# Keys, values and the sample's probabilities: transposed by TensorE, or in 32 by 32 blocks by VectorE with DMAs through DRAM

## The chip, the cores and the metric

The kernel runs on one core of a Trainium2 chip. The metric is device time in microseconds (us) of one execution. Engines are named as the profile names them: PE (TensorE's matmuls), PEld (its weight loads), DVE (VectorE), ACT (ScalarE), POOL (GpSimd), SP (SyncE, which only issues DMAs).

## What is computed

One layer of a decoder on 256 prompt tokens and 8 samples of 8 tokens, all of width 2048:

```
z = RMSNorm(x) @ W_in      # [B | C | h | q | k | v | gate_conv | gate_attn]
y_A = (B * conv3(C * h)) @ W_conv_out
y_B = attention(q, k, v) @ W_attn_out      # 16 query heads, 4 key/value heads of 64, window 128,
                                           # relative bias, a sink in the softmax's denominator
x = x + (sigmoid(gate_conv) * y_A + sigmoid(gate_attn) * y_B) @ W_o
x = x + SwiGLU(RMSNorm(x)); y = RMSNorm(x)
```

The prompt attends within itself; each sample attends to 128 cached keys and values and to its own 8 new ones. Besides y, the last 128 keys and values of the prompt and of each sample are outputs, row by row (a token's keys side by side).

## The kernel before, in words

The activations lie transposed, a feature to a partition and the 320 tokens along the row. Each weight matrix streams from DRAM in tiles of 128 x 1024 floats (four blocks of 128 rows by 256 columns; SP issues the loads, four buffers). Each weight tile is split into two parts, the upper one by ACT (whi, L129) and the lower one by DVE (wlo, L130), three buffers each, and gives PE 24 matmuls with 320 columns (L186, in the helper `product`): upper weights by upper activations, upper by lower, lower by upper. The order of the products is: keys and values together (L376), four of q, then four times C, H and B for the short convolution, then eight times gate_conv, gate_attn, W_conv_out and W_attn_out, then W_o, then the gate and up products and the down products.

Attention is side work. It is written as generators; `product` calls `tick` after each weight tile, and `tick` runs the generator to its next `yield`. So a `yield` puts what follows it behind one more weight tile of PE work (24 matmuls). The instructions that a tick emits stand behind the latest weight split and matmul on ACT, DVE and PE (`issue_after`); apart from that, a planner that works from its own estimates of durations puts each engine's instructions in order, so POOL's queue need not follow the order of the code. `nudge` (L207) is a single matmul whose result nobody uses.

While the q products run, `kv_work` runs: the first norm (`first_norm`, which scales vT and kT, L456), then `kv_natural` for three groups of tokens (128, 128, 64), a yield behind each, then `keys_twice`. `kv_natural(t)` turns values (L502) and, for the second and third group, keys (L505) from feature-major to token-major by PE: 2, 4 and 4 transpositions of 128 x 128 or 128 x 64 into the PSUM tile pk. DVE copies them out to vn (L506) and kn (L509), and POOL's queue issues DMAs of the outputs (L511 to L515). vn is then the stationary operand of the products of probabilities and values (L611 for the prompt, L726 for the sample's new tokens).

While C, H and B run, `attention` runs: the prompt's eight units, then the sample. The sample's probabilities lie in s_s (L701: divided by their sum), rows of heads and queries, for each sample 128 cached and 8 new keys. One tick takes a copy of the new part (pnew, L703). The next has eight PE transpositions of the cached part into spp (L709), copied by ACT to ptw (L710), one of the new part into spn (L712), copied by DVE to pns (L714), and then DVE spreads pns over the samples (ptn, L716). Two yields later PE multiplies by the new values (L726) and by the cached ones (L736) into spo, and a tick after that ACT and DVE take spo to at_t (L621, L622).

The convolution's small steps share POOL: copies into ue and out to g (L811, L812, L818, L819) and products with the norm (L829, L830). ACT (L822) and DVE (L824) do the rest of it.

Of the kernel before, what the change touches and what calls it, by code (L numbers as in the profile page):

```python
# [8 lines left out]
F32 = mybir.dt.float32  # L9
F32R = mybir.dt.float32r  # L10
AF = mybir.ActivationFunctionType
ALU = mybir.AluOpType
# [3 lines left out]
D = 2048  # L16
TP, NB, TS = 256, 8, 8
T = TP + NB * TS
DC = 1024
NH, NKV, HD, GRP = 16, 4, 64, 4  # L20
DKV = NKV * HD
WIN = 128
# [4 lines left out]
P = 128  # L27
# [21 lines left out]
TOK = [(0, 128), (128, 128), (256, 64)]  # L49
# [3 lines left out]
def hybrid_layer(ctx: ExitStack, tc: tile.TileContext, a: dict, o: list):  # L53
    nc = tc.nc
    y_0, y_r, nk_p, nv_p, nk_s, nv_s, ncv = o

    w_in, w_kv, w_co, w_ao, w_o, w_g, w_u, w_d = (
        a[n] for n in ("w_in", "w_kv", "w_conv_out", "w_attn_out", "w_o", "w_gate", "w_up", "w_down")
    )
# [7 lines left out]
    dr = ctx.enter_context(tc.tile_pool(name="dr", bufs=1, space=bass.MemoryType.DRAM))  # L67
# [4 lines left out]
    def ps_aux(name):  # L72
        return aux[0].tile([P, 512], F32, tag="aux", name=name)
# [3 lines left out]
    def u(s):  # L77
        uid[0] += 1
        return f"{s}_{uid[0]}"
# [133 lines left out]
    def flip(ap):  # L213

        *rest, (step, n) = ap.ap
        return bass.AP(ap.tensor, ap.offset + (n - 1) * step, [*rest, (-step, n)])


    ident = cst.tile([P, P], F32, name="ident")
    ones = cst.tile([P, 1], F32, name="ones")  # L220
# [8 lines left out]
    blk = cst.tile([64, NB], F32, name="blk")  # L229
# [47 lines left out]
    kT = zz.tile([P, 2, T], F32, name="kT")  # L277
    vT = zz.tile([P, 2, T], F32, name="vT")
    vn = [zz.tile([P, DKV], F32, name=f"vn{t}") for t in range(3)]
# [198 lines left out]
    pr = pr_p.enter_context(tc.tile_pool(name="pr", bufs=1, side="right"))  # L478
# [16 lines left out]
        return at_t[:, o:o + TP]  # L495


    def kv_natural(t):
        t0, tn = TOK[t]
        pk = ps_aux(u("pk"))  # L500
        for j in range(2):
            nc.tensor.transpose(pk[:tn, j * P:(j + 1) * P], vT[:, j, t0:t0 + tn], ident)  # L502
        if t > 0:
            for j in range(2):
                nc.tensor.transpose(pk[:tn, 256 + j * P:256 + (j + 1) * P], kT[:, j, t0:t0 + tn], ident)  # L505
        nc.vector.tensor_copy(vn[t][:tn, :], pk[:tn, 0:DKV])  # L506
        if t > 0:
            kn = pr.tile([P, 4, WIN], F32, tag="s", name=u("kn"), bufs=3).rearrange("p g k -> p (g k)")[:, :DKV]
            nc.vector.tensor_copy(kn[:tn, :], pk[:tn, 256:512])  # L509
            if t == 1:  # L510
                nc.gpsimd.dma_start(nk_p[0, 0].rearrange("t h d -> t (h d)"), kn)  # L511
                nc.gpsimd.dma_start(nv_p[0, 0].rearrange("t h d -> t (h d)"), vn[1])
            else:
                for dst, s in ((nk_s, kn), (nv_s, vn[2])):
                    nc.gpsimd.dma_start(  # L515
                        dst[0, :, WIN - TS:WIN].rearrange("b t h d -> b t (h d)"), s[:tn, :]
                    )

    def cache_shift():

# [128 lines left out]
    def sample_attention(sm):  # L649
        kf = sm.tile([P, NB, 2, W2], F32, name="kf")  # L650
        for h in range(0, NB, 2):
            nc.gpsimd.dma_start(kf[:, h:h + 2, :, 0:WIN], a["cache_kt"][:, h:h + 2])
        s = sm.tile([P, NB, W2], F32, name="s_s")
        yield
        new = kT[:, :, TP:T].rearrange("p j (b t) -> p b j t", b=NB)
        for j in range(2):
            nc.scalar.activation(kf[:, :, j, WIN:W2], new[:, :, j], AF.Copy)
        yield
        yield
        for base in range(0, NB, 3):  # L660
            ps = ps_aux(u("pss"))
            n = min(3, NB - base)
            for b in range(base, base + n):
                o0 = (b - base) * W2
                for kv in range(NKV):
                    j, par = kv // 2, kv % 2
                    rows = slice(par * 64, par * 64 + 64)
                    nc.tensor.matmul(
                        ps[kv * 32:(kv + 1) * 32, o0:o0 + W2], qs[rows, j, b, :], kf[rows, b, j, :],
                        start=True, stop=True,  # L670
                    )
            nc.vector.tensor_add(
                s[:, base:base + n, :], ps[:, 0:n * W2].rearrange("p (b k) -> p b k", b=n),
                flip(bias_s).unsqueeze(1).to_broadcast([P, n, W2]),
            )
        yield
        yield

        def vals(b):
            cv = sm.tile([P, DKV], F32, tag="ckv", name=u("cv"), bufs=8)  # L680
            nc.gpsimd.dma_start(cv, a["cache_v"][0, b].rearrange("t h d -> t (h d)"))
            return cv

        cvs = {b: vals(b) for b in range(NB)}
        mx = wk.tile([P, NB], F32, tag="smx", name="smx")
        den = wk.tile([P, NB], F32, tag="sden", name="sden")
        es = wk.tile([P, NB], F32, tag="ses", name="ses")
        nc.vector.tensor_reduce(mx, s, axis=AX.X, op=ALU.max)
        nc.vector.tensor_scalar(mx, mx, sink_s, -1.0, op0=ALU.max, op1=ALU.mult)
        nc.vector.tensor_scalar(es, mx, sink_s, None, op0=ALU.add)  # L690
        yield
        for b in range(NB):
            nc.scalar.activation(
                s[:, b, :], s[:, b, :], AF.Exp, bias=mx[:, b:b + 1], accum_out=den[:, b:b + 1]
            )
        nc.scalar.activation(es, es, AF.Exp)
        yield
        nc.vector.tensor_add(den, den, es)
        nc.vector.reciprocal(den, den)
        for b in range(NB):  # L700
            nc.vector.tensor_scalar(s[:, b, :], s[:, b, :], den[:, b:b + 1], None, op0=ALU.mult)  # L701
        pn = sm.tile([P, NB, TS], F32, name="pnew")
        nc.vector.tensor_copy(pn, s[:, :, WIN:W2])  # L703
        yield
        ptw = sm.tile([P, NB * P], F32, name="ptw")
        for h in range(2):
            pp = ps_aux(u("spp"))
            for i in range(4):
                nc.tensor.transpose(pp[:, i * P:(i + 1) * P], s[:, h * 4 + i, 0:WIN], ident)  # L709
            nc.scalar.activation(ptw[:, h * 512:(h + 1) * 512], pp, AF.Copy)  # L710
        pp = ps_aux(u("spn"))
        nc.tensor.transpose(pp[:64, 0:P], pn.rearrange("p b k -> p (b k)"), ident)  # L712
        pns = sm.tile([64, P], F32, name="pns")
        nc.vector.tensor_copy(pns, pp[:64, 0:P])  # L714
        ptn = sm.tile([64, NB, P], F32, name="ptn")
        nc.vector.tensor_tensor(  # L716
            ptn, pns.unsqueeze(1).to_broadcast([64, NB, P]), blk.unsqueeze(2).to_broadcast([64, NB, P]),
            op=ALU.mult,
        )
        yield  # L720
        yield
        pos = [ps_aux(u("spo")) for _ in range(2)]
        for j in range(2):
            for par in range(2):
                kv = j * 2 + par
                nc.tensor.matmul(  # L726
                    pos[j][par * 64:(par + 1) * 64, 0:256].rearrange("p (b r) -> p b r", b=NB),
                    vn[2][:64, kv * HD:(kv + 1) * HD], ptn[:, :, kv * 32:(kv + 1) * 32],
                    start=True, stop=False,
                )  # L730
        for b in range(NB):
            cv = cvs.pop(b)
            for j in range(2):
                for par in range(2):
                    kv = j * 2 + par
                    nc.tensor.matmul(  # L736
                        pos[j][par * 64:(par + 1) * 64, b * 32:(b + 1) * 32],
                        cv[:, kv * HD:(kv + 1) * HD], ptw[:, b * P + kv * 32:b * P + (kv + 1) * 32],
                        start=False, stop=(b == NB - 1),
                    )  # L740
        yield
        for j in range(2):
            src = pos[j][:, 0:256].rearrange("p (b g t) -> p g b t", b=NB, g=GRP)
            o = LEAD_A + j * 4 * at_row
            rows = at_t[:, o:o + 4 * at_row].rearrange("p (g w) -> p g w", g=GRP)[:, :, -2 * JS:]
            two_to(*(rows[:, :, c:c + JS].rearrange("p g (b t) -> p g b t", b=NB) for c in (0, JS)), src)
        yield
# [10 lines left out]

    def kv_work():
        yield from first_norm()  # L760
        for t in range(3):
            kv_natural(t)
            yield
        yield from keys_twice()

    def attention():
# [31 lines left out]
    for cp in range(4):  # L798
        c_sb = []
        ps = in_pair(O_C + cp * CW, "C")  # L800
        for c in range(2):
            t = tmp("ta", "csb")
# [4 lines left out]
        for c in range(2):  # L807
# [12 lines left out]
            cv = tmp("tc", "cv")  # L820
            n = UL - 2
# [11 lines left out]
        for c in range(2):  # L833
            ch = cp * 2 + c
            cv, cs = conv[c]
            t = tmp("td", "bc")
# [23 lines left out]
    for mp in range(8):  # L860
        c0 = mp * CW
        sg = {}
        for nm, off, tag in (("gc", O_GC, "ta"), ("ga", O_GA, "tb")):
            ps = in_pair(off + c0, nm)
            for c in range(2):
                t = tmp(tag, nm)[:, :T]
# [12 lines left out]
        for c in range(2):  # L879
            t = sg["ga", c]  # L880
# [394 lines left out]
```

## Time and profile before

| | |
|---|---|
| time, median of 3 runs | 1600.82 us (1600.62 to 1601.08) |
| profiled execution, first to last instruction | 1598.6 us |
| what lies around the span, by the median | 2.2 us |
| DVE busy | 884.0 us, 55% |
| ACT busy | 650.6 us, 41% |
| POOL busy | 78.3 us, 5% |
| HBM read and written | 253.30 MB, 5.08 MB |

The profile has no time of its own execution but its span; the median comes from runs without it. In rows of groups, "x8" is a count, then come the busy time of the group in us, the mean ns of one, and the idle time before them with what ended it. The chain in order of time lists, for each piece of the work that ended last, its start, its length, its engine, its output's name, its line and a count. DMA rows give KB each and the median us from issue to landing.

### The profile page before, as it was taken

How to read it: one execution, taken by the hardware profiler on the slowest of the kernel's cores; microseconds unless marked ns; L12 is line 12 of the kernel's file. 1: busy time of each engine (PE TensorE's matmuls, PEld its weight loads, DVE VectorE, ACT ScalarE, POOL GpSimd, SP SyncE). 2: the span in 40 equal slices, each digit the busy share in tenths (PEclk: the TensorE clock that was granted, in tenths of full speed). 3: DMA queues.
4: the chain of work that ended last, by engine and by line, in shares of the span. 5: the costliest groups of instructions: out<-in, count | busy, mean ns of one | idle time of the engine just before them, and what ended most of it. 6: DMA issues, size and time to landing. Idle time of an engine off the chain costs nothing.

```text
span 1598.6 us, 26406 instructions
## 1 busy us (share of the span) xinstructions
PE 1590.2 (99%) x10957; PEld 1554.8 (97%) x10957; DVE 884.0 (55%) x1315; ACT 650.6 (41%) x928; POOL 78.3 (5%) x123
## 2 busy tenths in 40 slices
PE   9999999999999999999999999999999999999998
PEld 9999999999999999999999999998888999999887
DVE  7879565445555545556555555553444455555556
ACT  7555433433333334444333333333333334444443
POOL 1101311000000003320000000000000000000000
PEclk9999999999999999999999999999999999999999
DMA  7554546545444444444445454455555445545552
GB/s 271 178 169 138 185 145 195 169 156 156 157 157 158 158 158 158 156 154 155 157 159 159 158 158 156 154 155 162 156 157 158 157 158 158 158 156 154 184 180 93
DMA packets 74399, 258.13 MB, mean 161 GB/s; under 512 B 8552, under 2 KB 11928, under 8 KB 74152
## 3 DMA queue, kind: packets, MB, share of 16 engines
q1 hardware_dynamic: 71880, 249.86, 49.4%
q0 software_dynamic: 1968, 5.90, 1.3%
q8 instruction: 86, 1.41, 0.4%
q10 hardware_dynamic: 432, 0.69, 0.1%
q14 instruction: 33, 0.27, 0.0%
HBM read 253.30 MB, written 5.08 MB: 162 GB/s over the span
## 4 chain that ended last, share of the span: by engine, by line
PE 99%; DVE 0%; ACT 0%; DVEq 0%; issue 0%
PE fu L186 18%; PE fg L186 18%; PE dn L970 9%; PE ga L186 7%; PE wo L186 7%; PE gc L186 7%; PE dn L978 6%; PE B L186 3%; PE C L186 3%; PE H L186 3%; PE q L186 3%; PE ya L186 3%; PE yc L186 3%; PE dl L974 2%; PE kv L376 2%; PE dn L1125 1%
## 5 line engine op out<-in xcount | busy, mean ns | idle before, releaser
L130 DVE TENSOR_TENSOR wlo<-wraw,whi 128x1024 fp32r<-128x1024 f32 (+1 forms) x460 | 561.7, 1222 | 585.4 <-ACT whi L129 470.0
L129 ACT ACTIVATE whi<-wraw 128x1024 fp32r<-128x1024 f32 (+1 forms) x460 | 485.5, 1056 | 720.4 <-PE fu L186 129.4
L186 PE MATMUL fu<-hh_t,whi 128*128 128x320 f32 x704 | 205.1, 301 | 0.0
L186 PE MATMUL fu<-hl_t,whi 128*128 128x320 f32 x704 | 205.1, 301 | 0.0
L186 PE MATMUL fg<-hl_t,whi 128*128 128x320 f32 x704 | 205.1, 301 | 0.0
L186 PE MATMUL fg<-hh_t,whi 128*128 128x320 f32 x704 | 205.1, 301 | 0.0
L186 PE MATMUL fu<-hh_t,wlo 128*128 128x320 f32 x704 | 158.9, 301 | 0.0
L186 PE MATMUL fg<-hh_t,wlo 128*128 128x320 f32 x704 | 158.9, 301 | 0.0
L970 PE MATMUL dn<-a_t,whi 128*128 128x512 f32 x640 | 155.4, 382 | 0.0
L186 PEld LDWEIGHTS fu<-hh_t,whi 128*128 128x128 f32 x704 | 131.8, 187 | 0.0
L186 PEld LDWEIGHTS fg<-hh_t,whi 128*128 128x128 f32 x704 | 131.8, 187 | 0.0
L186 PEld LDWEIGHTS fu<-hl_t,whi 128*128 128x128 f32 x704 | 131.8, 187 | 0.0
L186 PEld LDWEIGHTS fg<-hl_t,whi 128*128 128x128 f32 x704 | 131.8, 187 | 0.0
L970 PEld LDWEIGHTS dn<-a_t,whi 128*128 128x128 f32 x640 | 115.5, 187 | 16.3 <-issue 0.9
L186 PEld LDWEIGHTS fu<-hh_t,wlo 128*128 128x128 f32 x704 | 116.2, 187 | 0.0
L186 PEld LDWEIGHTS fg<-hh_t,wlo 128*128 128x128 f32 x704 | 116.2, 187 | 0.0
L978 PEld LDWEIGHTS dn<-a_t,wlo 128*128 128x128 f32 x640 | 97.7, 188 | 6.9
L978 PE MATMUL dn<-a_t,wlo 128*128 128x320 f32 x640 | 103.4, 301 | 0.0
L186 PE MATMUL wo<-m_l,whi 128*128 128x320 f32 x256 | 74.6, 301 | 0.0
L186 PE MATMUL ga<-xl_t,whi 128*128 128x320 f32 x256 | 74.6, 301 | 0.0
L186 PE MATMUL gc<-xl_t,whi 128*128 128x320 f32 x256 | 74.6, 301 | 0.0
L186 PE MATMUL wo<-m_h,whi 128*128 128x320 f32 x256 | 74.6, 301 | 0.0
(312 smaller groups left out, 2659.0 us busy)
## 6 DMA issues: line engine op xcount, KB each, us to landing
wraw<-in_w_in_dram SPq DMA_DIRECT2D x128, 512.0 KB, 3.8
wraw<-in_w_gate_dram SPq DMA_DIRECT2D x88, 512.0 KB, 3.7
wraw<-in_w_up_dram SPq DMA_DIRECT2D x88, 512.0 KB, 3.7
wraw<-in_w_down_dram SPq DMA_DIRECT2D x88, 512.0 KB, 3.7
wraw<-in_w_o_dram SPq DMA_DIRECT2D x32, 512.0 KB, 3.8
wraw<-in_w_conv_out_dram SPq DMA_DIRECT2D x16, 512.0 KB, 3.7
wraw<-in_w_attn_out_dram SPq DMA_DIRECT2D x16, 512.0 KB, 3.6
wraw<-in_w_kv_dram SPq DMA_DIRECT2D x6, 512.0 KB, 7.5
```

The costliest lines, as they stand in the source:

```text
L129: last["hi"] = nc.scalar.activation(hi, src, AF.Copy)
L130: last["lo"] = nc.vector.tensor_sub(lo, src, hi.bitcast(F32))
L186: last["mm"] = nc.tensor.matmul(turns(fives(ps[c][:, :T])), w[:, k, c * P:(c + 1) * P], turns(x(kc)), start=(kc == 0 and i == 0), stop=(kc ...
L376: last["mm"] = nc.tensor.matmul(turns(fives(ps[c][:, :T])), w[:, k, c * P:(c + 1) * P], turns(x(kc)), start=(kc == 0 and m == 0), stop=(kc ...
L970: nc.tensor.matmul(turns(placed(ps[c])), parts[k][0][:, cs], turns(a_move(k)), start=k == 0, stop=False)
L974: nc.tensor.matmul(low, a_low(k), parts[k][0], start=k == 0, stop=k == nf - 1 and c0 < E0)
L978: last["mm"] = nc.tensor.matmul(turns(placed(ps[c])[:, :, 0:JT]), parts[k][1][:, cs], turns(a_move(k)[:, :, 0:JT]), start=False, stop=k == ...
L1125: nc.tensor.matmul(turns(placed(ps[c])[:, :, JR:]), held[k][0][:, cs], turns(a_move(k)[:, :, JR:]), start=k == 0, stop=k == nf - 1,)
```

## The change

`kv_natural` is one generator for all tokens. DVE turns the values of the 256 prompt tokens (one instruction, 512 elements in a row), the keys of the last 192 tokens (384) and the values of the 64 sample tokens (128) in blocks of 32 by 32. A yield later the blocks go to a scratch in DRAM (one write for each of two tiles) and come back with each block in its place, 8 reads for each tile, all issued from POOL's queue by the new helper `blocks_out`. Two yields after that POOL copies the keys into the order of the outputs, and the four outputs are sent as before. The columns of the value weights are put in another order on the host, so that the values come back in the right order without a copy.

The sample's probabilities are turned in the same way: DVE turns the new part (64 elements) and the cached part (1024) in the tick that takes the copy pnew, and two writes and six reads go through DRAM into pns and ptw. Four yields stand between this and ptn, where one stood between pnew and the transpositions before. ptw is laid out by key/value head.

Nineteen PE transpositions, the PSUM tiles pk, spp and spn, five copies of pk and one of spn on DVE, and two copies of spp on ACT go away.

```diff
+    def blocks_out(dst, src, name="scr"):
+        scr = dr.tile(list(src.shape), F32, tag=f"scr{src.shape[1] * src.shape[2]}", name=u(name), bufs=2)
+        nc.gpsimd.dma_start(scr, src)
+        for b, to in enumerate(dst):
+            nc.gpsimd.dma_start(to, scr[:, b].rearrange("(a i) m -> i a m", a=4))
...
-    def kv_natural(t):
-        t0, tn = TOK[t]
-        pk = ps_aux(u("pk"))
-        for j in range(2):
-            nc.tensor.transpose(pk[:tn, j * P:(j + 1) * P], vT[:, j, t0:t0 + tn], ident)
-        if t > 0:
-            for j in range(2):
-                nc.tensor.transpose(pk[:tn, 256 + j * P:256 + (j + 1) * P], kT[:, j, t0:t0 + tn], ident)
-        nc.vector.tensor_copy(vn[t][:tn, :], pk[:tn, 0:DKV])
...
+    def kv_natural():
+        x1, x2 = (
+            pr.tile([P, 3, 2 * WIN], F32, tag="pT", name=u("x"), bufs=4).rearrange("p a b -> p (a b)")[:, :512].rearrange(
+                "p (b m) -> p b m", m=64
+            ) for _ in range(2)
+        )
+        def turned(x, src):
+            nc.vector.transpose(
+                x.rearrange("p b (j f) -> p j b f", j=2), src.rearrange("p j (b t) -> p j b t", t=32)
+            )
+        turned(x1, vT[:, :, 0:TP])
+        turned(x2[:, 0:6], kT[:, :, P:T])
+        turned(x2[:, 6:8], vT[:, :, TP:T])
+        yield
...
+        blocks_out([part(t, b) for t in range(2) for b in range(4)], x1)
+        blocks_out([*(part(3, b) for b in range(4)), *(part(t, b) for t in (4, 2) for b in range(2))], x2)
+        yield
+        yield
+        for t, tn in ((0, P), (1, TS * NB)):
+            nc.gpsimd.tensor_copy(
+                kn[t][:tn, :DKV].rearrange("p (j a f) -> p a j f", j=2, a=4),
+                kn[t][:tn, DKV:].rearrange("p (a j f) -> p a j f", j=2, a=4),
+            )
...
         nc.vector.tensor_copy(pn, s[:, :, WIN:W2])
-        yield
-        ptw = sm.tile([P, NB * P], F32, name="ptw")
-        for h in range(2):
-            pp = ps_aux(u("spp"))
-            for i in range(4):
-                nc.tensor.transpose(pp[:, i * P:(i + 1) * P], s[:, h * 4 + i, 0:WIN], ident)
-            nc.scalar.activation(ptw[:, h * 512:(h + 1) * 512], pp, AF.Copy)
-        pp = ps_aux(u("spn"))
-        nc.tensor.transpose(pp[:64, 0:P], pn.rearrange("p b k -> p (b k)"), ident)
-        pns = sm.tile([64, P], F32, name="pns")
-        nc.vector.tensor_copy(pns, pp[:64, 0:P])
+        spare_k = kf.rearrange("p b j k -> p (b j k)")
+        xn = spare_k[:, 0:64].rearrange("p (b m) -> p b m", b=2)
+        xw = spare_k[:, 64:64 + NB * P].rearrange("p (b m) -> p b m", b=4)
+        pns = sm.tile([64, 4, 32], F32, name="pns")
+        ptw = sm.tile([P, NKV, NB * 32], F32, name="ptw")
+        nc.vector.transpose(xn, pn.rearrange("p b k -> p (b k)").rearrange("p (b k) -> p b k", b=2))
+        nc.vector.transpose(
+            xw.rearrange("p b (n j) -> p n b j", n=NB), s[:, :, 0:WIN].rearrange("p n (b k) -> p n b k", b=4)
+        )
+        blocks_out([pns[32 * b:32 * b + 32] for b in range(2)], xn)
+        blocks_out([ptw[32 * b:32 * b + 32] for b in range(4)], xw)
+        yield
+        yield
+        yield
+        yield
         ptn = sm.tile([64, NB, P], F32, name="ptn")
...
-                        cv[:, kv * HD:(kv + 1) * HD], ptw[:, b * P + kv * 32:b * P + (kv + 1) * 32],
+                        cv[:, kv * HD:(kv + 1) * HD], ptw[:, kv, b * 32:(b + 1) * 32],
...
-        for t in range(3):
-            kv_natural(t)
-            yield
+        yield from kv_natural()
+        yield
         yield from keys_twice()
...
+    values = w[:, o_k + DKV:o_gc].reshape(D, NKV, 2, 32).transpose(0, 2, 1, 3).reshape(D, DKV)
+    inputs["w_kv"] = by_block(_np.concatenate([w[:, o_k:o_k + DKV], values], axis=1), 2 * DKV)
```

More of the change, by code (lines that the diff above doesn't have):

```diff
@@ L495, in q2 @@
         return at_t[:, o:o + TP]
-    def kv_natural(t):
-        t0, tn = TOK[t]
-        pk = ps_aux(u("pk"))
-        for j in range(2):
-            nc.tensor.transpose(pk[:tn, j * P:(j + 1) * P], vT[:, j, t0:t0 + tn], ident)
-        if t > 0:
-            for j in range(2):
[L505 to L517, printed above, removed]
+    def kv_natural():
[12 more added lines that the diff above has]
+        yield
+        kn = [pr.tile([P, 4, WIN], F32, tag="s", name=u("kn"), bufs=3).rearrange("p g k -> p (g k)") for _ in range(2)]
+        rows = [x.rearrange("p (a m) -> p a m", m=64) for x in (*vn, *(x[:, DKV:] for x in kn))]
+        part = lambda t, b: rows[t][32 * b:32 * b + 32]
+        blocks_out([part(t, b) for t in range(2) for b in range(4)], x1)
[7 more added lines that the diff above has]
+            )
+        nc.gpsimd.dma_start(nk_p[0, 0].rearrange("t h d -> t (h d)"), kn[0][:, :DKV])
+        nc.gpsimd.dma_start(nv_p[0, 0].rearrange("t h d -> t (h d)"), vn[1])
+        for dst, s in ((nk_s, kn[1][:, :DKV]), (nv_s, vn[2])):
+            nc.gpsimd.dma_start(
+                dst[0, :, WIN - TS:WIN].rearrange("b t h d -> b t (h d)"), s[:TS * NB, :]
+            )
@@ L703, in sample_attention @@
         nc.vector.tensor_copy(pn, s[:, :, WIN:W2])
-        yield
-        ptw = sm.tile([P, NB * P], F32, name="ptw")
-        for h in range(2):
-            pp = ps_aux(u("spp"))
-            for i in range(4):
-                nc.tensor.transpose(pp[:, i * P:(i + 1) * P], s[:, h * 4 + i, 0:WIN], ident)
-            nc.scalar.activation(ptw[:, h * 512:(h + 1) * 512], pp, AF.Copy)
-        pp = ps_aux(u("spn"))
-        nc.tensor.transpose(pp[:64, 0:P], pn.rearrange("p b k -> p (b k)"), ident)
-        pns = sm.tile([64, P], F32, name="pns")
-        nc.vector.tensor_copy(pns, pp[:64, 0:P])
+        spare_k = kf.rearrange("p b j k -> p (b j k)")
[6 more added lines that the diff above has]
+            xw.rearrange("p b (n j) -> p n b j", n=NB), s[:, :, 0:WIN].rearrange("p n (b k) -> p n b k", b=4)
+        )
+        blocks_out([pns[32 * b:32 * b + 32] for b in range(2)], xn)
+        blocks_out([ptw[32 * b:32 * b + 32] for b in range(4)], xw)
+        yield
+        yield
+        yield
+        yield
         ptn = sm.tile([64, NB, P], F32, name="ptn")
         nc.vector.tensor_tensor(
-            ptn, pns.unsqueeze(1).to_broadcast([64, NB, P]), blk.unsqueeze(2).to_broadcast([64, NB, P]),
-            op=ALU.mult,
+            ptn, pns.rearrange("p a j -> p (a j)").unsqueeze(1).to_broadcast([64, NB, P]),
+            blk.unsqueeze(2).to_broadcast([64, NB, P]), op=ALU.mult,
         )
@@ L1251 @@
     inputs["w_in"] = by_block(_np.concatenate([w[:, :o_q], w[:, o_q + heads], w[:, o_gc:]], axis=1))
-    inputs["w_kv"] = by_block(w[:, o_k:o_gc], 2 * DKV)
+    values = w[:, o_k + DKV:o_gc].reshape(D, NKV, 2, 32).transpose(0, 2, 1, 3).reshape(D, DKV)
+    inputs["w_kv"] = by_block(_np.concatenate([w[:, o_k:o_k + DKV], values], axis=1), 2 * DKV)
     inputs["w_attn_out"] = by_block(_np.asarray(inputs["w_attn_out"])[0][heads])
```

## The prediction

> **What bounds the kernel now.** I read the page first (span, busy shares, chain), then who waited on PE, then the chain in order of time around the two places that change, then the queues of DVE, ACT and POOL there.
>
> ```profile
> span 1598.6 us, 26406 instructions
> PE 1590.2 (99%) x10957; PEld 1554.8 (97%) x10957; DVE 884.0 (55%) x1315; ACT 650.6 (41%) x928; POOL 78.3 (5%) x123
> PE 99%; DVE 0%; ACT 0%; DVEq 0%; issue 0%
> ```
>
> PE is busy all the time, and the chain that ends last is PE from end to end. The view of PE's waits has one row, and that lies at the start:
>
> ```profile
> PE wm L309 <- PEq L1258: 0.8, 1, 0.8
> ```
>
> So PE waits for no weights, no transposed keys and no probabilities. An instruction taken off PE is gained in full; work given to DVE, POOL or DMA queues costs nothing until it makes PE late. The medians of the runs are 2.2 us above this span (1600.82 against 1598.6); my sum uses differences only, so I set it on the median.
>
> The chain in order of time (start, length, what) at the keys and values, then at the sample's probabilities:
>
> ```profile
> 50.28 0.22 PE pk L502 x2
> 50.50 3.37 PE q L186 x24
> 53.87 0.22 PE pk L502 x2
> 54.09 0.22 PE pk L505 x2
> 54.31 3.37 PE q L186 x24
> 57.67 0.22 PE pk L502 x2
> 57.89 0.22 PE pk L505 x2
> 58.11 3.37 PE q L186 x24
> ```
>
> ```profile
> 193.33 7.03 PE C L186 x48
> 200.35 10.24 PE H L186 x72
> 210.60 0.87 PE spp L709 x8
> 211.47 0.11 PE spn L712
> 211.58 3.38 PE H L186 x24
> 221.31 10.29 PE B L186 x72
> 231.60 13.44 PE C L186 x96
> ```
>
> The lengths say two things. Each transposition takes 0.11 us of PE. And the product's matmuls run in two rhythms: 13.44/96 = 140.0 ns each from 231.60 on, 10.24/72 = 142.2 ns between 200.35 and 210.60. The slow one isn't the clock, which is 1.00 there (window, span, busy time of PE, PEld, DVE, ACT and POOL, granted clock, DMA share, GB/s):
>
> ```profile
> 196.00:211.00 15.00, 15.00 (x109) 15.00 (x108) 7.94 (x19) 8.31 (x22) 0.00 (x0) 1.00 0.40 125
> ```
>
> A block of other matmuls between two weight tiles can leave either rhythm, and it then lasts until the next such block: the slow one that began at 193 ends at the transpositions at 210.60.
>
> **What goes.** Ten transpositions of kv_natural (2 + 4 + 4) and nine of the sample: 5 x 0.22 + 0.87 + 0.11 = 2.08 us, all on the chain. That is minus 2.08. Off the chain go five copies of pk on DVE, the copy of spn, and two copies of spp on ACT.
>
> **What DVE gets.** No row shows a 32 by 32 transposition. The nearest are elementwise rows by size, and the dearest row per element is the reciprocal:
>
> ```profile
> L783 DVE SCALAR_TENSOR_TENSOR qs<-q,rb 128x64 f32<-128x64 f32 x8 | 1.7, 215 | 0.0
> L559 DVE TENSOR_TENSOR w<-ps,bias 128x512 f32<-128x512 f32 x8 | 5.5, 685 | 0.0
> L130 DVE TENSOR_TENSOR wlo<-wraw,whi 128x1024 fp32r<-128x1024 f32 x53 | 64.7, 1223 | 39.1 <-ACT whi L129 36.5 <-PE spp L709 2.2
> L244 DVE RECIPROCAL r<-r 128x320 f32<-128x320 f32 x1 | 2.2, 2153 | 0.5 <-ACT r L243 0.5
> ```
>
> Keys and values: 512, 384 and 128 elements, about 0.69 + 0.55 + 0.28 = 1.5 us at the elementwise rate. They stand where the first copy of vn stood (0.4 us), so the lower weight parts behind them end 1.1 us later:
>
> ```profile
> 51.81 0.41 DVE L506 COPY vn<-pk 128x256 f32<-128x256 f32 x1
> 52.14 2.35 DVE L130 TENSOR_TENSOR wlo<-wraw,whi 128x1024 fp32r<-128x1024 f32 x2
> 55.27 0.30 PE L186 MATMUL q<-xh_t,wlo 128*128 128x320 f32 x1
> ```
>
> One lower part belongs to each weight tile; counted forward to where the order has settled, the first of the two at 52.14 is the one that PE reads at 55.27. It ends at about 53.36, so the slack is 1.9 us, and 1.1 fits in it. The later copies that go give the time back. At the reciprocal's 6.7 ns per element the 1024 elements would take 6.9 us, and PE would be late by 6.9 - 0.4 - 1.9 = 4.6 us. Below nothing there is no gain, since PE doesn't wait here. I take the elementwise rate, as the operation is one pass over the data, and 0 for PE. The sample's 64 and 1024 elements (about 1.4 us, at 206) stand in a stage where the weight parts run two tiles, 7 us, ahead: 0, and 0.3 us at the dear rate.
>
> **What POOL and the queues get.** Keys and values: 2 writes to the scratch and 16 reads back, two POOL copies, the four outputs as before. Sample: 2 writes and 6 reads. Each read waits on POOL for its write to land, and whatever POOL has next stands behind it.
>
> ```profile
> L681 POOL DMA_DIRECT2D cv<-in_cache_v_dram x8 | 4.3, 541 | 1.5 <-DMA kf<-in_cache_kt_dram 1.3 <-issue 0.2
> L652 POOL DMA_DIRECT2D kf<-in_cache_kt_dram x4 | 3.0, 760 | 0.1
> e_scr<-e_sb POOLq DMA_DIRECT2D x1, 24.0 KB, 2.2
> kf<-in_cache_kt_dram POOLq DMA_DIRECT2D x4, 256.0 KB, 5.0
> 101.76 0.74 POOL L532 DMA_DIRECT2D bias<-e_scr  x1 [6.07 <-DVE s L562]
> 142.43 0.44 PE L611 MATMUL po<-pT,vn 128*64 128x256 f32 x2
> ```
>
> An issue costs 0.54 to 0.76 us, a landing 2.2 to 5.0. At the dear ends, nothing overlapped, the keys and values take 18 x 0.76 + 3 x 5.0 = 28.7 us from about 53: done by 82. PE first reads vn at 142.43 and POOL has nothing else until the bias load at 101.76, so this is hidden, with at least 20 us to spare. The traffic (1 MB, beside weights that fill half of the DMA time) delays no weight, as the eight cv loads and four kf loads of the sample delay none now.
>
> In the sample part the first block can be turned at 206.4 and both are by about 207.8:
>
> ```profile
> 206.19 0.19 DVE L703 COPY pnew<-s_s 128x64 f32<-128x64 f32 x1
> ```
>
> Cheap ends: write, land, issue the reads, land: PE's copies are there by about 216. They are needed later than now: four yields stand where none stood and one goes, so the product of probabilities and values moves three weight tiles back: the block of 3.0 us that now ends at 221.31 starts at about 221.3 - 3.0 + 3 x 3.36 - 1.0 = 227.4. The dear ends, all in series, give 206.6 + 2 x (0.76 + 5.0) + 1.5 + 3.0 + 5.0 = 227.6. Hidden, at the worst but for 0.2 us.
>
> **What moves.** With the transpositions at 210.60 gone, the slow rhythm that starts at 193.33 runs on to about 227: 120 matmuls more at 2.2 ns, plus 0.27 us. Keys doubled (keys_twice) come one tile later, still inside the q products; the prompt's scores, which read them, come after those.
>
> **Sum.** 1600.82 - 2.08 + 0.27 = 1599.0, minus 0.11%.
>
> **Rivals.** *The rhythm after the sample block is the slow one (slower).* Between that block and the next interruption of the stream PE runs nothing but weight tiles:
>
> ```profile
> 715.74 0.15 PE nudge L207
> ```
>
> After the block come 288 matmuls (last C, H, B), 2304 of the merge, 768 of W_o, 96 of the first gate: 3456. In the slow rhythm each costs 2.22 ns more: 7.7 us, so 1606.7. Now the block is entered in the fast rhythm and left in it (221.31). After the change it is entered in the slow one, three tiles later, at the end of a product. Whether a block leaves the fast or the slow rhythm shows in the 24 matmuls behind it, 3.36 to 3.38 us or 3.41 to 3.42. The first and the last of the 13 tiles that stand behind blocks between 111 and 168 us:
>
> ```profile
> 111.28 3.37 PE H L186 x24
> 164.75 3.42 PE H L186 x24
> ```
>
> Of these 13, four are slow (119.17, 139.08, 145.83, 164.75). With the blocks at 171 (fast after it), 191 (slow), 211 and 218 (fast) it is 5 of 17. For it speaks that the block's place and entry change; against it that a block ended four of the five slow entries (at 122, 149, 171 and 210). It decides at the first tile after the block: 3.42 there means 1606.7.
>
> *POOL's waits hold the convolution and with it the weights.* Behind the sample's reads on POOL stand the conv copies and products (L818 to L830, from 214.22).
>
> ```profile
> 214.22 0.18 POOL L818 COPY g<-ue 128x2 f32<-128x2 f32 x1 [30.80 <-DVE ue L813]
> ```
>
> ```profile
> L822 ACT ACTIVATE cv<-ue,xv 128x336 f32<-128x336 f32 x2 | 1.2, 578 | 3.2 <-POOL g L819 2.5 <-DVE ue L814 0.7
> ```
>
> By the second row ACT's conv step was released once by POOL's g, and the weight splits stand behind it on ACT. Dear ends in series: 206.6 + 0.76 + 5.0 + 1.5 + 0.76 + 5.0 + 3.0 = 222.6 until POOL is free, 224.7 until the next upper part is split; the tile that needs it, the third of B, starts at about 211.58 + 3.38 + 2 x 3.36 - 1.0 = 220.7. PE would be late by 4.0 us: 1603.0. Against it: cheap ends free POOL at about 213.5, before 214.22. The Trainium skill, page "SBUF — State Buffer", section "SBUF: two separate sides", says that POOL can't write a DMA's descriptors while DVE runs an SBUF copy on two ports, which would lengthen this chain. The eight cv issues above, at 541 ns each, show no such hold.
>
> *The transpositions cost PE what their rows list (faster).* The listed length of one is 0.27 us:
>
> ```profile
> L709 PE MATMUL spp<-ident,s_s x8: 271/273/273, 210.4 to 211.2; 128*128 128x128 f32 x8
> ```
>
> If that were what PE loses, 19 x 0.272 = 5.2 us would go: 1600.82 - 5.2 + 0.3 = 1595.9. Against it: the same eight start within 0.8 us, and the chain gives them 0.87 together. The Trainium skill, page "TensorE: Matmul & The Clock Gate", section "Part 4: PE-mode transpose", gives about 275 ns for a transposition in a kernel's context. The trace agrees as to the listed length, not as to the step from one to the next, 0.11.
>
> **How the numbers follow.** What a measurement of this kernel can tell from no change is about 0.2%, 3.2 us; the forecast lies within it. Forecast 0.57, slow rhythm 0.28 (near 5 of 17), POOL or DVE makes PE late 0.10 (1599 to 1603.9, of which 0.07 count as the same), full cost of transpositions 0.05. Faster 0.05, same 0.64, slower 0.31. The forecast's own range is 1598.0 to 1599.6: less if the block at 191 and those of the prompt happen to leave the fast rhythm (0.54 for the stretch to 227, and some 0.4 for the slow tiles of the prompt), more by small waits. To hold 8 in 10 the range must reach the slow rhythm: 1598.0 to 1606.9.
>
> **What will show it.** No pk, spp or spn rows on PE; PE's waits still without a row behind the start (a wait of PE on wlo or whi at 55 or 221 would be DVE or POOL being late; one on ptn, ptw or vn would be the scratch); the tile behind the sample block at 3.36 to 3.38, and 13.44 per 96 matmuls up to 715 (13.65 would be the slow rhythm). A transposition of 1024 elements on DVE at 1.2 us. I am wrong if PE's chain isn't 2 us shorter up to 231, or if the rhythm differs.

## The result, and the profile after

After the change the median of six runs is 1606.71 us, that of the kernel before on the same chip 1600.87 us: a ratio of 1.0031, 95% interval 1.0021 to 1.0041. The change costs 5.8 us, and the forecast of 1599.0 us was wrong. The time is that of the prediction's first rival, 1606.7. The runs after the change fall in two groups: five lie between 1606.48 and 1607.55, one at 1599.77, where the forecast was. The profile is of the run of 1606.48.

The engines' line of the page, and PE's waits in full. Beside 1590.2 us before, PE is busy 5.6 us longer, with 19 matmuls fewer:

```profile
PE 1595.8 (99%) x10938; PEld 1559.7 (97%) x10938; DVE 884.3 (55%) x1314; ACT 650.3 (41%) x926; POOL 94.7 (6%) x151
```

```profile
PE wm L316 <- PEq L1284: 0.8, 1, 0.8
PE kv L383 <- ACT whi L129: 0.2, 1, 0.2
```

PE waits for nothing that the change added (the second row is the keys' and values' product at the start). So no wait took the 5.8 us. The chain in order of time, at the keys and values and then at the sample's probabilities:

```profile
40.04 20.18 PE q L186 x144
60.22 0.15 PE nudge L207
```

```profile
192.18 7.03 PE C L186 x48
199.20 13.65 PE H L186 x96
212.86 13.66 PE B L186 x96
226.51 1.01 PE spo L752 x8
...
229.51 13.85 PE C L186 x96
243.36 13.65 PE H L186 x96
```

The transpositions are gone in both places. The H and B products run at 13.65/96 = 142.2 ns a matmul up to the block of spo, as forecast. Behind the block they go on so: the first group of 96 takes 13.85 us (0.2 of that is PE's start behind a block: before, the 72 matmuls behind the block took 10.29, and 72 x 140.0 is 10.08), and the next 13.65, where before stood 13.44. The chain further on, at the nudge of the first interruption of the stream, which stood at 715.74 before (two small matmuls of 0.15 us each come right ahead of it in both):

```profile
721.53 0.15 PE nudge L207
```

From the C product behind the block to this matmul passed 715.74 - 231.60 = 484.14 us before and 721.53 - 229.51 = 492.02 us after, 7.88 more; up to that C product the kernel is 231.60 - 229.51 = 2.09 us ahead. The difference, 5.79 us, is the result but for 0.4 us: the profiled span grew by 6.2 us, from 1598.6 to 1604.8, and the medians differ by 5.84. The same in one view, the windows (span, busy time and count of PE, PEld, DVE, ACT and POOL, granted clock, DMA share, GB/s), before and after:

```profile
231.00:715.00 484.00, 484.00 (x3459) 484.00 (x3458) 247.70 (x294) 186.46 (x217) 39.67 (x40) 1.00 0.50 161
```

```profile
231.00:715.00 484.00, 484.00 (x3405) 484.00 (x3405) 242.78 (x287) 184.49 (x212) 40.16 (x40) 1.00 0.48 157
```

In equal time, with PE busy throughout and the granted clock 1.00 in both, PE does 54 matmuls fewer: 484/3459 = 139.9 ns each before, 142.1 after. That stretch holds nothing that the change touched. A reader who looks only at busy shares or waits sees no difference; it shows in the counts.

The starts of the single matmuls in the two traces show that both rhythms are steady. Between 240 and 700 us nearly all steps before are 140 ns. After, the steps repeat every nine matmuls: 143, 142, 142, 143, 142, 141, 144, 141 and 142 ns, together 1280 ns, all the way from 236 to 721 us. So the loss isn't made of single stalls; every step is longer.

The Trainium skill, page "TensorE: Matmul & The Clock Gate", section "Back-to-back issue gap", gives N/2.4 + 2.5 ns as the gap of an isolated matmul at full clock, worked out 135.8 ns for 320 columns (an estimate). No run here has isolated matmuls of that width; the stream of weight loads and matmuls has two spacings, 140.0 and 142.2, both above that, at a granted clock of 1.00 both times.

What VectorE got, by groups (count, busy us, mean ns of one):

```profile
L732 DVE STREAM_TRANSPOSE kf<-s_s 128x1024 f32<-128x1024 f32 x1 | 1.2, 1245 | 0.0
L514 DVE STREAM_TRANSPOSE x<-vT 128x512 f32<-128x512 f32 x1 | 0.7, 703 | 0.0
L514 DVE STREAM_TRANSPOSE x<-kT 128x384 f32<-128x384 f32 x1 | 0.5, 539 | 0.0
L514 DVE STREAM_TRANSPOSE x<-vT 128x128 f32<-128x128 f32 x1 | 0.3, 271 | 0.0
L731 DVE STREAM_TRANSPOSE kf<-pnew 128x64 f32<-128x64 f32 x1 | 0.2, 208 | 0.0
```

They run at the elementwise rate: (1245 - 703)/512 = 1.06 ns for each further element, beside (1223 - 685)/512 = 1.05 in the prediction's elementwise rows. The way through DRAM, as POOL's queue shows it at the end of the keys' and values' part and at the sample's:

```profile
71.32 0.59 POOL L537 DMA_DIRECT2D out_dram<-vn  x1
```

```profile
211.70 0.57 POOL L224 DMA_DIRECT2D ptw<-scr  x1 [3.68 <-DMA scr<-kf]
...
214.99 0.20 POOL L843 COPY g<-ue 128x2 f32<-128x2 f32 x1
```

The first part is done by 72 us, PE first reads vn at 141. At the second POOL waits 3.68 us for the write to land and is free at 215.0. DVE's queue holds a wait that the prediction didn't price:

```profile
217.28 1.22 DVE L742 TENSOR_TENSOR ptn<-pns,blk 64x1024 f32<-64x1024 f32 x1 [3.32 <-DMA pns<-scr]
...
218.90 1.21 DVE L130 TENSOR_TENSOR wlo<-wraw,whi 128x1024 fp32r<-128x1024 f32 x1
```

DVE stands 3.32 us for the copy of pns to come back, and a weight part stands behind it. Here PE isn't held by that; in three of the experiments it is (e5_entry, e7_earlier, e8_both), by 0.2 to 0.3 us.

### The profile page after: what moved, and what is told of

It is laid out like the page before. It is cut to its first block, busy times and chain, and to the rows that moved or that the text cites. A ratio compares the mean times of both kernels' runs of the same rounds, so it can differ in the third digit from the quotient of the medians.

```text
span 1604.8 us, 26408 instructions
## 1 busy us (share of the span) xinstructions
PE 1595.8 (99%) x10938; PEld 1559.7 (97%) x10938; DVE 884.3 (55%) x1314; ACT 650.3 (41%) x926; POOL 94.7 (6%) x151
## 4 chain that ended last, share of the span: by engine, by line
PE 99%; DMA 1%; ACT 0%; DVE 0%; SPq 0%; issue 0%; DVEq 0%; ACTq 0%
PE fg L186 18%; PE fu L186 18%; PE dn L995 9%; PE ga L186 7%; PE wo L186 7%; PE gc L186 7%; PE dn L1003 6%; PE C L186 3%; PE ya L186 3%; PE yc L186 3%; PE B L186 3%; PE H L186 3%; PE q L186 3%; PE dl L999 2%; PE kv L383 1%; PE dn L1150 1%
## 5 line engine op out<-in xcount | busy, mean ns | idle before, releaser
L186 PE MATMUL ga<-xh_t,whi 128*128 128x320 f32 x256 | 75.3, 303 | 0.0
L186 PE MATMUL gc<-xh_t,whi 128*128 128x320 f32 x256 | 75.3, 303 | 0.0
```

The costliest lines, as they stand in the source:

```text
L186: last["mm"] = nc.tensor.matmul(turns(fives(ps[c][:, :T])), w[:, k, c * P:(c + 1) * P], turns(x(kc)), start=(kc == 0 and i == 0), stop=(kc ...
```

## The experiments

**Theory.** The block of spo is entered in the slow rhythm, because the transpositions that used to end that rhythm are gone; it leaves PE in it, and 3456 matmuls pay 2.22 ns each. **Added work**, a rival: the added traffic and DVE's and POOL's work slow PE. **Place**, another rival: the block's new place, behind the last B instead of inside it, sets the rhythm. Later a third question: does the entry alone decide?

Each ratio is against the kernel before on the same chip, whose median was 1600.56 us for e1 to e4, 1600.66 for e5 to e8 and 1600.68 for e9 to e12; "in" and "out" are the rhythms ahead of and behind the block of spo in the profiled run:

| kernel | median us (lowest to highest, runs) | ratio to before, 95% | in, out |
|---|---|---|---|
| before | 1600.87 (1600.09 to 1601.08, 6) | 1 | fast, fast |
| after | 1606.71 (1599.77 to 1607.55, 6) | 1.0031, 1.0021 to 1.0041 | slow, slow |
| e1_nudge | 1599.37 (1598.87 to 1600.71, 11) | 0.9993, 0.9985 to 1.0002 | slow, slow |
| e2_usual | 1599.39 (1598.94 to 1601.02, 11) | 0.9994, 0.9985 to 1.0002 | slow, slow |
| e3_kv_only | 1599.00 (1598.71 to 1600.27, 11) | 0.9992, 0.9983 to 1.0000 | fast, fast |
| e4_sample_only | 1607.58 (1607.26 to 1614.09, 6) | 1.0056, 1.0043 to 1.0069 | slow, slow |
| e5_entry | 1599.02 (1598.24 to 1600.70, 10) | 0.9991, 0.9982 to 1.0000 | fast, fast |
| e6_later | 1607.26 (1606.77 to 1608.78, 4) | 1.0043, 1.0029 to 1.0057 | slow, slow |
| e7_earlier | 1606.51 (1598.49 to 1611.79, 10) | 1.0025, 1.0008 to 1.0042 | slow, slow |
| e8_both | 1599.31 (1598.49 to 1601.08, 11) | 0.9992, 0.9984 to 1.0001 | fast, fast |
| e9_kv_twice | 1598.60 (1598.26 to 1599.12, 11) | 0.9987, 0.9978 to 0.9996 | fast, fast |
| e10_before_nudges | 1601.20 (1600.83 to 1601.54, 11) | 1.0003, 0.9994 to 1.0012 | fast, slow |
| e11_no_turns | 1607.58 (1607.02 to 1608.10, 4) | 1.0043, 1.0029 to 1.0056 | slow, slow |
| e12_best | 1598.79 (1598.36 to 1599.24, 11) | 0.9988, 0.9979 to 0.9997 | fast, fast |

**e1_nudge: after, with one matmul into an unused tile ahead of the last H product.**

```diff
+        if cp == 3:
+            nudge(xh, xl)
         ps = in_pair(O_H + cp * CW, "H")
```

> The changed kernel with one nudge matmul ahead of the last H product, one product behind the sample block. Rhythm (PE's matmuls run at 142.2 instead of 140.0 ns from the sample block at 229 us to the gate product at 715): only the C product stays slow, then 140.0, so 1606.7 - 7.7 + 0.2 + 0.1 = 1599.3 us. Rival, added work (the scratch DMAs, POOL's waits or the DVE transpositions cost the 7 us): a nudge takes none of it away, 1606.8 us.

1599.37 us, 7.3 us less than after (7.0 less when each is taken against before on its own chip). The chain in order of time, with the nudge at the gate as its last line:

```profile
229.60 13.85 PE C L186 x96
243.45 0.15 PE nudge L207
243.59 13.44 PE H L186 x96
...
714.30 0.14 PE nudge L207
```

The block is left in the slow rhythm as in the kernel after, and one matmul of 0.15 us ends it. All the traffic and all the work of the change are still there. From the C product to the nudge at the gate pass 714.30 - 229.60 = 484.70 us, 7.32 less than the 492.02 of after; 3360 matmuls at 2.22 ns less, and one matmul of 0.15 us more, would be 7.31. So the loss is the rhythm, and a rhythm can be ended from outside.

**e2_usual: the same place, a matmul that reads the activations in the order of the products.** The nudge reads its operands straight. Here the moving operand and the output have the access pattern of the products.

```diff
+        if cp == 3:
+            x0 = xl(0)
+            nc.tensor.matmul(
+                turns(fives(ps_aux(u("usual"))[:, :T])), bass.AP(x0.tensor, x0.offset, [list(x0.ap[0]), [1, P]]),
+                turns(xh(0)), start=True, stop=True,
+            )
```

> The same with a matmul of the products' own access pattern (rows read as 16 x 5 x 4) in place of the nudge, which reads one run of 320. If any interruption of the stream resets the rhythm: 1599.3 us, as with the nudge. If only the nudge's straight read does: 1606.8 us, C, H and all behind at 13.65 us per 96 matmuls. Rival, added work: 1606.8 us with products at 13.44.

1599.39 us, and the same chain:

```profile
243.54 0.14 PE usual L832
243.68 13.44 PE H L186 x96
```

The straight read isn't what ends the rhythm. One more matmul with the products' own pattern in the stream is enough.

**e3_kv_only: keys and values by VectorE and DRAM, the sample by PE as before.**

> Only the keys and values turned by DVE and sent through DRAM (18 of the 26 scratch DMAs); the sample's probabilities by PE as before. Rhythm: the sample block is entered in the fast rhythm behind the PE transpositions and left in it, so 1600.87 - 1.10 = 1599.8 us. Rival, added work: most of the traffic and of POOL's waits are here, so at least half of the loss shows, 1603 us or more.

1599.00 us, 1.56 less than before. Ten transpositions at 0.11 are 1.10; the other 0.46 is not accounted for. The chain has the transpositions at 209.74, and the block is left fast:

```profile
220.46 10.29 PE B L186 x72
230.75 13.44 PE C L186 x96
```

**e4_sample_only: the other half, the sample alone.**

> Only the sample's probabilities turned by DVE and sent through DRAM, keys and values by PE as before. Rhythm: the block is entered in the slow rhythm at the same place and left in it, 1600.87 - 0.98 + 0.27 + 7.7 = 1607.9 us. Rival, added work: a third of the DMAs, 1602 us or so.

1607.58 us. The chain behind the block:

```profile
230.78 13.85 PE C L186 x96
244.63 13.65 PE H L186 x96
```

The loss is in the sample's half; the keys' and values' half gains. Two of the six runs took 1612.82 and 1614.09, for which no theory had a number. They are 5 to 6 us above the others. The slow rhythm kept up from 715 to 1080 as well would give 365 x 2.22/140 = 5.8 us, but no trace of such a run is there, so that is only an estimate.

**e5_entry: after, with the matmul of e1 one product group earlier (`cp == 2`), so that the block of spo is entered in the fast rhythm at its new place.**

> The changed kernel with one nudge ahead of the third H product (at 199 us), so that the sample block at 226 us is entered in the fast rhythm, and nothing behind it. If the rhythm at entry decides how the block is left: fast behind it, 1599.4 - 0.6 = 1598.7 us. If the block's place in the weight stream (end of a product) decides: slow behind it, 1598.7 + 7.7 = 1606.4 us. If neither decides and it is chance from run to run: times of both sizes.

1599.02 us, none of the ten runs above 1600.70. The chain in order of time:

```profile
199.02 0.15 PE nudge L207
...
212.32 5.48 DMA pns<-scr
...
220.78 5.89 PE B L186 x40
226.67 1.01 PE spo L752 x8
...
229.67 13.65 PE C L186 x96
243.31 13.44 PE H L186 x96
```

Behind the block 13.65 is 13.44 and the 0.2 us of the start; 13.44 follows. With the same place, the same traffic and a fast entry, the block is left fast. The chain leaves PE at 212.32, which the chain of after never does: the landing of pns, 5.48 us, then ptn and a weight part on DVE, then PE. PE's waits have a row for it:

```profile
PE B L186 <- DVE wlo L130: 0.3, 1, 0.3
```

**e6_later and e7_earlier: the block one tile later (inside the last C) and one earlier (inside the last B, as before the change).** The diff is that of e6_later; e7_earlier has one yield less there instead.

```diff
         yield
+        yield
         ptn = sm.tile([64, NB, P], F32, name="ptn")
```

> The changed kernel with one yield more ahead of ptn: the block comes one weight tile later, behind the first tile of the last C, still entered in the slow rhythm. If the rhythm at entry decides: 1606.7 us as before. If the place decides: the block is inside a product again, as in the kernel before, and 1599.3 us is as likely.

> The changed kernel with one yield less: the block comes one weight tile earlier, behind the third tile of B, entered in the slow rhythm. Entry decides: 1606.7 us. Place decides: 1599.0 us is as likely.

e6_later took 1607.26 us, e7_earlier 1606.51. The chains behind the block, of e6_later and of e7_earlier:

```profile
232.88 10.44 PE C L186 x72
243.32 13.65 PE H L186 x96
```

```profile
226.16 3.61 PE B L186 x24
229.77 13.65 PE C L186 x96
```

Both are slow: 10.44 for 72 (the 72 behind the block in the kernel before took 10.29), then 13.65. A block in the middle of a product, even of the same product as before, is left slow too when it is entered slow. So the place doesn't set the rhythm. Three of the ten runs of e7_earlier took 1598.49 to 1599.67, though: there is chance in it from one execution to the next. In its trace DVE waits 4.07 us for pns, and PE loses about 0.3 us to a lower weight part ahead of the block (the chain goes through DVE there). Whether this differs between runs isn't shown; only the profiled one can be read.

**e8_both: matmuls at `cp > 1`, that is those of e5 and e1 together.**

> The changed kernel with a nudge ahead of the third and of the fourth H product. Rhythm: slow from 192 to 199 us, fast to the sample block, at worst slow for one product behind it: 1600.6 - 2.1 - 0.2 + 0.3 + 0 to 0.2 = 1598.6 to 1598.9 us, under both kernels and in every run. Rival, added work: 1606 us.

1599.31 us, 0.4 to 0.7 more than expected, and not less than e5_entry. PE's waits show 0.2 us for a lower weight part there. The entry being fast, the second matmul has nothing to end.

**e10_before_nudges: the same two matmuls in the kernel before.**

> The kernel before with the two nudges of e8_both. The nudge is no gain by itself where the rhythm is fast already: 1600.6 - 0.2 (fast from 200 instead of 211 us) + 0.3 (two matmuls) = 1600.7 us. If nudges helped whatever the rhythm: 1599.3 us or less.

1601.20 us, no gain. The chain in order of time shows a miss of the theory:

```profile
214.85 3.36 PE B L186 x24
218.21 1.01 PE spo L726 x8
...
221.21 10.44 PE B L186 x72
231.65 13.66 PE C L186 x96
245.31 0.14 PE nudge L207
245.45 13.45 PE H L186 x96
```

The block is entered fast (3.36 for 24) and left slow (10.44, 13.66), and only the second matmul ends it. So the entry doesn't settle the exit. Over the 14 profiles: entered slow, the block of spo is left slow in 7 of 7; entered fast, left fast in 6 of 7. The times of the runs without a profile agree. Five kernels enter the block slow in their profile and have nothing behind it that ends the rhythm before 715 (after, e4, e6, e7, e11): 26 of their 30 runs took 1606.40 us or more, four took 1598.49 to 1599.77. Five enter it fast and have nothing behind it either (before, e3, e5, e9, e12): none of their 132 runs took more than 1601.31. The entry tips it; it isn't a law.

**e11_no_turns: the kernel before with the sample's nine PE transpositions left out and nothing in their place.** ACT and DVE copy the probabilities as they lie, so the sample's attention is computed with unturned probabilities. No DVE transposition, no scratch, the block at its old place.

```diff
-            pp = ps_aux(u("spp"))
-            for i in range(4):
-                nc.tensor.transpose(pp[:, i * P:(i + 1) * P], s[:, h * 4 + i, 0:WIN], ident)
-            nc.scalar.activation(ptw[:, h * 512:(h + 1) * 512], pp, AF.Copy)
+            nc.scalar.activation(ptw[:, h * 512:(h + 1) * 512], s[:, h * 4:(h + 1) * 4, 0:WIN], AF.Copy)
...
-        nc.vector.tensor_copy(pns, pp[:64, 0:P])
+        nc.vector.tensor_copy(pns, s[:64, 0, 0:P])
```

> The kernel before without the sample's nine PE transpositions: ptw and pns are copied from the probabilities as they lie, so the sample's attention is left unturned; no scratch, no DVE transposition, no DMA more, and the block at its old place. If the entry in the slow rhythm is the cause: 1600.6 - 1.0 + 0.3 + 7.7 = 1607.6 us in most runs. If the added work is: 1599.6 us.

1607.58 us in four runs of four. Less work, and slower than before by 6.9 us:

```profile
214.22 3.42 PE B L186 x24
...
220.63 10.44 PE B L186 x72
231.07 13.65 PE C L186 x96
```

This decides against the rival of the added work. Without any of the added instructions and transfers, at the old place, the loss is there in full: it comes from taking nine matmuls off PE.

**e12_best: after, with the matmul of e5 and ptn two yields later (six ahead of it, none behind), the block where it is in after.**

```diff
         yield
         yield
+        yield
+        yield
         ptn = sm.tile([64, NB, P], F32, name="ptn")
...
-        yield
-        yield
         pos = [ps_aux(u("spo")) for _ in range(2)]
...
+        if cp == 2:
+            nudge(xh, xl)
         ps = in_pair(O_H + cp * CW, "H")
```

> The changed kernel with a nudge ahead of the third H product (the block is then entered in the fast rhythm) and ptn two yields later, so that DVE doesn't wait for pns with the weight splits behind it. Rhythm: fast before and behind the block in every run, and no wait of PE on wlo: 1600.6 - 2.1 - 0.2 + 0.1 = 1598.4 us, below both kernels.

1598.79 us, a ratio of 0.9988 (0.9979 to 0.9997): the change with its two side effects mended is faster than both kernels, by 1.9 us (0.12%) against before, a small gain whose interval stays just below 1. The chain is PE from end to end again:

```profile
198.95 0.14 PE nudge L207
199.09 13.45 PE H L186 x96
212.54 13.44 PE B L186 x96
225.98 1.01 PE spo L752 x8
```

From the matmul to the block pass 27.03 us, in e5_entry 226.67 - 199.02 = 27.65: the wait for pns had cost PE 0.62 us there. In the medians that is 0.23 us, too little to tell.

**e9_kv_twice: e12_best with the keys' and values' writes and reads through the scratch made twice** (2 writes and 16 reads more).

> The kernel of e12_best with the scratch traffic of the keys and values made twice (2 writes and 16 reads more). If that traffic and POOL's waits are hidden: 1598.4 us, no difference from e12_best. Rival, added work costs: more by the time of 18 issues and two landings, up to 15 us.

1598.60 us, beside 1598.79 for e12_best, with overlapping ranges. The way through DRAM is hidden, as priced.

## Why the prediction was wrong

- **What goes: right.** From 40.18 to 61.48 passed 21.30 us before and from 40.04 to 60.22 20.18 after: 1.12 less, forecast 1.10. Up to the C product behind the block the kernel is 2.09 us ahead; 0.2 of that is the start behind the block, which now falls behind this point, so 1.9 beside the sum's 2.08 - 0.27 = 1.81. The prediction's third rival (0.272 each, 5.2 us) is out.
- **What DVE gets: right.** 703, 539 and 271 ns against 690, 550 and 280, and 1245 + 208 = 1.45 us against "about 1.4". PE waits for no weight behind them.
- **What POOL and the queues get: right in time, wrong in who waits.** The first part was done by 72 us (bound 82). POOL was free at 215.0 and held nothing that PE waited for (the prediction's second rival: out). The eight cv issues could show no hold by a DVE copy, though: between 177 and 184 us, where they lie, DVE ran no copy. But the reads' landing was weighed against PE's need at 227 alone. ptn runs on DVE, which is two weight tiles ahead of PE: it came up at about 214, and pns landed at 217.3. Behind it stood weight parts. In the kernel after this cost PE nothing visible, in e5_entry 0.62 us (by e12_best, where ptn comes later).
- **What moves: right.** The block starts at 226.5 (forecast 227.4), and the slow rhythm runs on to it, at 142.2 ns a matmul.
- **The step that failed** is the weight between the forecast and its first rival: "it is 5 of 17", hence 0.57 for a block left fast and 0.28 for one left slow. So the sum put the rhythm behind the block at nothing, where 7.7 us stood: the runs showed that this block, entered slow, is left slow (7 of 7 profiles, and 26 of 30 runs by their time). The mechanism, the place where it decides, the count of 3456 matmuls and the price were as written: 7.88 us measured, less the 0.2 of the start, against 7.7. That 1606.71 us falls on 1606.7 to the hundredth is luck; the five runs there spread over 1.1 us.
- **Why the count misled.** It put together blocks of different make. Two of them have a habit: over the 14 profiles the scores' block at 190 is entered fast and left slow every time, and the last block of the prompt at 171 is entered slow and left fast every time. Those of the prompt between 110 and 160 have none: the slow tiles stand at 119, 139 and 146 in the profile before and at 123, 127, 154 and 157 in that of e10_before_nudges, with the same code up to there. The block of spo with a slow entry doesn't occur in the profile before, so no row there gave its chance. A count split by entry would have misled too: of the 17 blocks one of five slow entries was left slow, and four of twelve fast ones. It took a run with this block entered slow to tell.

What stays open: why a block leaves one rhythm or the other. Entry tips the block of spo (13 of 14 profiles), e10_before_nudges is the exception, and single runs of after (one of six) and of e7_earlier (three of ten) took the time of a fast rhythm with the same program. The three runs at 1611.79 to 1614.09 stay without a trace.

## What to carry to other kernels

- Where PE never waits, time can still hide in the spacing of its matmuls. Divide the chain's pieces by their counts on both sides of each interruption, and ask of every matmul that is taken out what its presence ended; then weigh that for the block at hand, not by a count over all blocks.
- Where thousands of matmuls follow one small block, try a single dummy matmul (0.15 us) behind it. In this kernel such a matmul met the slow rhythm eight times (e1_nudge, e2_usual, e5_entry, e8_both, e9_kv_twice, e12_best, twice in e10_before_nudges) and ended it each time; in e1_nudge it saved 7.3 us. Ahead of the block it is less sure: e10_before_nudges was entered fast and left slow all the same. It is worth nothing where the stream is fast already.
- A delay counted in PE's tiles isn't one on an engine that runs ahead of PE. Count a landing against the queue in which the waiting instruction stands.

## What the runs showed of the hardware that was not expected

- A stream of 128 x 128 weights with 320 columns kept one of two spacings, 140.0 ns (before) or 142.2 ns (after, nine steps in 1280 ns), for 3456 matmuls (484 and 492 us), at a granted clock of 1.00 and with PE busy throughout. One more matmul of 0.14 to 0.15 us, with either of the two access patterns tried, ended the slow one.
- Taking nine matmuls out of such a stream, with nothing put in their place, made the kernel 6.9 us slower (e11_no_turns).
